# Seven products in every block pair, alternating groups, and derived factors made ahead into DRAM, in a split-weight decoder trunk

## The chip, the cores and the metric

The kernel runs on one core of a Trainium2 chip. The metric is the device time of one execution in microseconds; the time given is the median of several runs.

## The reference

Two decoder layers over 256 tokens of width 2048, all in float32:

```python
for layer in range(2):
    mix = short_conv_mixer(h, ...)        # layer 0: gated convolution of width 3, w_in 2048x6144, w_out 2048x2048
    # layer 1: latent attention, 16 heads, with low-rank projections, rotary part and output projection w_o
    h = layer_norm(ALPHA * h + mix, ...)
    f = jnp.square(jax.nn.relu(h @ w1[layer])) @ w2[layer]     # w1 2048x8192, w2 8192x2048
    h = layer_norm(ALPHA * h + f, ...)
```

The two MLPs hold most of the work: each multiplies by 2048x8192 and by 8192x2048.

## The kernel before, in words

**Weights in two parts.** To keep float32 accuracy, each weight is used as the sum of a high and a low part. SP loads it in tiles of 128x1024 (512 KB) into a ring of five (`RAW`), ScalarE copies it into the high part (L127), VectorE subtracts that from the weight and gets the low part (L128). High and low parts live in two rings of eight (`WA`). A product (`dot`, L300 to L303) is then three matmuls: high by high, low by high, high by low.

All weights form one list, `stream`, in the order in which they are used. `take` hands out the next of it and runs the preparation (`prepare`, a generator of one step for a plain tile and three for a unit of a seven-product pair) a few steps ahead (`LOOK` = 5). The instructions are written in this way and then put in order for each engine by a scheduler; each engine works through its own queue in order.

**The MLP.** The 8192 hidden columns are worked in eight groups q. In each q, `products` computes eight blocks of 128 hidden columns for all 256 tokens (L215, L219), their squares follow, and the second half of q, "down", multiplies them by the q's 1024 rows of w2. In the first and the last q, this is plain. In the six between (`FAST`), hidden blocks are taken in pairs and token halves too, which gives products of 2x2 blocks, and such a product is done in seven multiplications instead of eight (a form of Strassen and Winograd, `fast_products`). The left factors S1 to S4 are made from the hidden blocks (L707 to L710). The right factors T1 to T4 are made from the weights: a unit is two raw tiles, holding blocks 11 and 22, 21 and 12. VectorE derives T1 and T3 together into a third tile (L162, 128x1024), then T2 (L166) and T4 (L169, both 128x512), and all of them are split as above.

The 2048 output columns of w2 form two groups of two column blocks. In group 0 all four pairs of a q are seven-product pairs; in group 1, worked first, the pairs are `MIXED = "sssp"`: three seven-product pairs and a plain one of eight products.

**The sums.** Each group has its sums of products, kept in SBUF between the q's and in eight PSUM banks while they are worked: ScalarE copies a sum into its bank before the products (`resumed`, L612) and back afterwards (`put_back`, L616); some are added into SBUF by VectorE (`keep`, L624) instead. `fold` puts the parts together at the end.

**Around the MLPs.** Ahead of the first stand the opening (first tiles of x and of w_in, loaded as `lead` and `first`, split a piece at a time), the rest of w_in with the convolution (`cbuf`, whose edges GpSimd clears, L557), and w_out; between the MLPs, the latent projections, attention and w_o. GpSimd does hardly anything else.

Of the kernel before, what the change touches and what calls it, by code (L numbers as in the profile page):

```python
# [10 lines left out]
F32 = mybir.dt.float32  # L11
F32R = mybir.dt.float32r
AF = mybir.ActivationFunctionType
ALU = mybir.AluOpType
# [22 lines left out]
FAST = range(1, NQ - 1)  # L37
MIXED = "sssp"
EVEN = (QC - 1, "22")
FIRST = (0, 1, 2, 3, 4, 6, 8, 12, 16)  # L40
# [5 lines left out]
LAG = 8  # L46
WO_G = 3
BEHIND = (2, 2, 2, 3, 2, 2, 3)

# [4 lines left out]
def trunk(ctx: ExitStack, tc: tile.TileContext, xT, vecs, lead, w_first, w_in, w_out, w_kv, w_q, w_uk, w_uv,  # L54
# [18 lines left out]
    def halves(w):  # L73

        lead = len(w.shape) - 2
        return [(w,)] if lead == 0 else [h for i in range(w.shape[0]) for h in halves(w[i])]

    stream = []
    for m in range(NC):
# [19 lines left out]
    stream += halves(w_o) + mlp_stream(1)  # L99

    class Banks:
# [39 lines left out]
    def prepare(i):  # L141

        if len(stream[i]) == 1:
# [4 lines left out]
            return  # L148
        r1, r2 = (load_raw(f"{i}_{j}", src) for j, src in enumerate(stream[i]))
        out = []  # L150

        def finished(r, name):
            hi, lo = parts(name)
            split(hi, lo, tiled(r))
            out.append((hi, lo))

        b22, (b21, b12) = r1[:, BW:], (r2[:, :BW], r2[:, BW:])
        finished(r1, f"{i}_1")
# [10 lines left out]
        nc.vector.tensor_tensor(t4, b21, b12, ALU.subtract)  # L169
        f = state["fast"].tile([P, 2, BW], F32R, tag="t4", name=f"t4_{i}", bufs=2)  # L170
        split(f[:, 0, :], f[:, 1, :], t4)
        b1, t13, b2 = ([[v.rearrange("p b c -> p (b c)")[:, o:o + BW] for v in w] for o in (0, BW)] for w in out)
        ready[i] = {"11": b1[0], "22": b1[1], "21": b2[0], "T2": b2[1], "T1": t13[0], "T3": t13[1],
                    "T4": [f[:, 0, :], f[:, 1, :]]}
        yield
# [7 lines left out]
    def take(halves=2, look=LOOK):  # L183

        i = state["next"]
        state["next"] += halves
        ahead = -sum(size(j) for j in range(i, i + halves))
        for j in range(i, len(stream)):
            for step in range(size(j)):
                ahead += 1  # L190
                if ahead > look:
                    return [ready.pop(i + k) for k in range(halves)]
# [6 lines left out]
        return [ready.pop(i + k) for k in range(halves)]  # L199

# [87 lines left out]
    def products(n, x, turned=None, banks=(None,)):  # L288

        for i in range(n):  # L290
            w = take()
            ps = psum("ps_u", banks[i % len(banks)])
            mm_run([(w, ps)], x, 0, NC, NC, turned=None if i else turned)
            yield ps
# [47 lines left out]

    def fast_products(ps, x, forms, j, fresh, ready, onto=()):

# [157 lines left out]

    def summed(ln, pss, add, m0=0):

        for m, ps in enumerate(pss, m0):
            add(ps, m)
            ln.count(m)
            ln.wide(m)
# [37 lines left out]
    pss = chain(opening(xhl), lagged(3 * NC - HEAD, xhl))  # L546
    ln = Norm(0, ALPHA)
    for m in range(NC):
        part = []
# [18 lines left out]
        if m >= NC // 2:  # L568
            for k in range(2 * m - NC, 2 * m - NC + 2):
                ln.prepare(k)  # L570
    nc.sync.dma_start(id_t, ident)
    ln.widen("a1", "a2")
    summed(ln, chain(products(1, z), lagged(NC - 1, z)), residual)

    def mlp(idx, ln, blocks, fast, begin=None, extra=None, last=False):
# [39 lines left out]
        def put_back(p, g, ps):  # L615
            nc.scalar.copy(place(p, g), ps)  # L616
# [9 lines left out]
        def resume(busy, free, ps, m):  # L626

            b2, b3, b4, b6 = free
            b1, b5, b7, b22 = busy
            for p, bank in {3: (("3", b3),), 4: (("2", b2),), 5: (("4", b4), ("1", b1)), 6: (("6", b6), ("5", b5)),  # L630
                            7: (("7", b7), ("22", b22))}.get(m, ()):
                ps[p] = resumed(p, 1, f"ps_r{p}", bank)

        def down_pairs(h, forms, busy, free, ps):

            b2, b3, b4, b6 = free
            b1, b5, b7, b22 = busy
            new = set(OWN) if q == FAST[0] else set()
            onto = set(ps) - new
            for j, kind in enumerate(MIXED):  # L640
                if kind == "s":
                    last = j == MIXED.rindex("s")
                    fast_products(ps, h, forms, j, new if j == 0 else (), OWN if last else (), onto)
                    if last:
                        for p in OWN:
                            put_back(p, 1, ps[p])
                        then = {p: resumed(p, 0, f"ps_f{p}", bank) for p, bank in (("3", b1), ("1", b5))}
                    continue
                for two in (((0, "2"), (1, "4")), ((1, "22"), (0, "3"))):
                    w, = take(1, LOOK + 1)  # L650
                    for t, p in two:
                        for kk in range(2):
                            k = 2 * j + kk
                            dot(ps[p], wide_rows(w, kk), held(h[k], t), False, k == QC - 1, (k, p) == EVEN, True)
                    if j == len(MIXED) - 1:
                        if "5" not in then:
                            then.update({p: resumed(p, 0, f"ps_f{p}", bank) for p, bank in (("5", b7), ("7", b6))})
                        for _, p in two:
                            put_back(p, 1, ps[p])
            n = QC // 2  # L660
            onto = set(then) - new
            then.update({p: psum(f"ps_f{p}", bank) for p, bank in (("2", b2), ("6", b4), ("4", b22))})
            for j in range(n):
                fast_products(then, h, forms, j, set(then) - onto if j == 0 else (), then if j == n - 1 else (), onto)
            for p, _, _ in FACTORS:
                (put_back if p in onto or p in new else keep)(p, 0, then[p])
            return (b3, b1, b5, b7), (b6, b2, b4, b22)

# [16 lines left out]

        busy, free = (0, 1, 2, 3), (4, 5, 6, 7)
        for q in range(NQ):
# [54 lines left out]
            else:  # L742
                folds = fold()
                begun = {}
                for m, ps in enumerate(products(QC, xhl, TURNED, busy)):
                    hidden(m, ps, whole)
                    if extra and m == 0 and q <= NB:
                        for t in range(2):
                            extra(block, q - 1, t, busy[2 + t])
                    if q in FAST:  # L750
                        resume(busy, free, begun, m)
                    if q == NQ - 1:
                        next(folds, None)
                        if last and m >= QC - 2:
                            for t in range(2):
                                last_sum(m - QC + 2, t, free[2 * (m - QC + 2) + t])
                        if begin:
# [15 lines left out]
            else:  # L773
                busy, free = down_pairs(h, forms, busy, free, begun)

# [28 lines left out]


    with tc.tile_pool(name="att", bufs=1) as ap:
        lat = act.tile([P, 2 * NK, 2 * T], F32R, tag="c", name="lat")
# [92 lines left out]
        with tc.tile_pool(name="att2", bufs=2) as a2, \  # L900
# [107 lines left out]
            for s, n in enumerate(BEHIND, H - 4):  # L1008
                together(s)
                for _ in range(n):  # L1010
                    next(outs)
# [8 lines left out]
    after.widen("a1", "a2")  # L1020
    summed(after, out_chunks(), residual)

# [165 lines left out]
```

## Time and profile before

| | |
|---|---|
| median of 3 runs | 2000.02 us (1996.99 to 2000.58) |
| profiled execution, span | 1994.9 us |
| matmuls (records) | 11110, busy 1987.7 us |
| VectorE busy | 1709.4 us, 86% |
| ScalarE busy | 1354.9 us, 68% |
| moved by DMA | 385.85 MB, mean 193 GB/s |

The profile gives the span of the execution that it recorded; what lies around it is not given, and the median of the timed runs is 5.1 us above it. The stages, in microseconds of that execution: opening from 5, rest of w_in and convolution from 28, w_out from 273, first MLP from 362 (its six `FAST` q's from 453, 83 each), latent projections and attention from 1044, w_o from 1205, second MLP from 1304 (its `FAST` q's from 1395, 84 each) to the end. A line of the timeline reads: start, duration, engine, line of the code, operation, output and input tiles, shape; in brackets how long the engine was idle before and what ended that.

### The profile page before, as it was taken

Reading aid. Unit: us, or ns where it says so; the run is one execution under the profiler, and the core shown is the slowest. Engines: PE = TensorE matmul, PEld = TensorE weight load, DVE = VectorE, ACT = ScalarE, POOL = GpSimd, SP = SyncE. Lnnn points to the kernel's source line nnn. Section 1 sums busy time; section 2 is a strip of 40 time slices with the busy share of each in tenths; the row PEclk is TensorE's granted clock in tenths of the full one; section 3 lists DMA queues with packets and bytes.
Section 4 is the critical chain, followed back from the end, with each engine's and each line's share of the span. In section 5 each row is a group of like instructions: output and inputs, shape, how many; then the busy total and the mean of one; then the engine's idle time right before and its main releaser. Section 6 shows DMA issues by size and latency. Waiting matters only on the chain.

```text
span 1994.9 us, 30180 instructions
## 1 busy us (share of the span) xinstructions
PE 1987.7 (100%) x11110; PEld 1737.2 (87%) x11110; DVE 1709.4 (86%) x2555; ACT 1354.9 (68%) x2154; POOL 2.3 (0%) x21
## 2 busy tenths in 40 slices
PE   9999999999999999999999999999999999999998
PEld 8888888988888888888889998898888888888886
DVE  8667667797999989989978988777899999999985
ACT  6444445586778778777756755558677787887772
POOL 0000000000000000000000000000000000000000
PEclk9999999999999999999999999999999999999999
DMA  8666666565657466574855543656464656656483
GB/s 318 205 191 187 190 190 190 179 193 157 212 170 251 148 216 221 177 243 147 281 171 159 170 140 123 201 180 195 146 233 155 232 161 220 222 178 233 150 269 130
DMA packets 106853, 385.85 MB, mean 193 GB/s; under 512 B 11857, under 2 KB 12625, under 8 KB 106449
## 3 DMA queue, kind: packets, MB, share of 16 engines
q1 hardware_dynamic: 106560, 383.79, 59.5%
q8 instruction: 87, 1.43, 0.3%
q14 instruction: 62, 0.50, 0.1%
q10 hardware_dynamic: 144, 0.13, 0.0%
HBM read 381.78 MB, written 2.10 MB: 192 GB/s over the span
## 4 chain that ended last, share of the span: by engine, by line
PE 98%; DVE 1%; ACT 1%; issue 0%; DVEq 0%; ACTq 0%
PE ps_u L215 20%; PE ps_l L215 13%; PE ps_u L219 10%; PE ps_l L219 7%; PE ps_f L300 4%; PE ps_f L303 4%; PE ps_f L302 4%; PE ps_r L303 4%; PE ps_r L302 4%; PE ps_r L300 4%; PE ps_d L300 2%; PE ps_d L302 2%; PE ps_d L303 2%; PE ps_w L249 2%; PE ps_w L248 2%; PE ps_w L247 2%
## 5 line engine op out<-in xcount | busy, mean ns | idle before, releaser
L128 DVE TENSOR_TENSOR lo<-raw,hi 128x1024 fp32r<-128x1024 f32 x710 | 861.8, 1220 | 190.6 <-ACT hi L127 119.9
L127 ACT CAST hi<-raw 128x1024 fp32r<-128x1024 f32 x710 | 741.8, 1051 | 247.4 <-PE ps_l L215 98.1
L215 PE MATMUL ps_u<-xhl,hi 128*128 128x512 f32 x1792 | 621.7, 392 | 0.0
L219 PE MATMUL ps_u<-xhl,lo 128*128 128x256 f32 x1792 | 498.2, 279 | 0.0
L215 PEld LDWEIGHTS ps_u<-xhl,hi 128*128 128x128 f32 x1792 | 334.5, 187 | 73.6 <-ACT acc L595 0.2
L219 PEld LDWEIGHTS ps_u<-xhl,lo 128*128 128x128 f32 x1792 | 338.1, 189 | 1.8
L215 PE MATMUL ps_l<-xhl_a,hi 128*128 128x512 f32 x704 | 244.1, 393 | 0.0
L219 PE MATMUL ps_l<-xhl_a,lo 128*128 128x256 f32 x704 | 195.4, 279 | 0.0
L215 PEld LDWEIGHTS ps_l<-xhl_a,hi 128*128 128x128 f32 x704 | 132.1, 188 | 29.9
L219 PEld LDWEIGHTS ps_l<-xhl_a,lo 128*128 128x128 f32 x704 | 131.9, 188 | 0.2
L127 ACT CAST hi_t<-raw_t 128x1024 fp32r<-128x1024 f32 x84 | 88.5, 1054 | 45.8 <-DVE raw_t L162 41.4
L162 DVE TENSOR_TENSOR raw_t<-raw,raw 128x1024 f32<-128x1024 f32 x84 | 102.3, 1218 | 1.8 <-DMA raw<-in_w2f_dram 1.5
L128 DVE TENSOR_TENSOR lo_t<-raw_t,hi_t 128x1024 fp32r<-128x1024 f32 x84 | 102.4, 1219 | 0.2
L718 ACT ACTIVATE fp<-fp 128x256 f32<-128x256 f32 x96 | 40.0, 416 | 63.2 <-DVE fp L356 62.6
L215 PE MATMUL ps_l<-z,hi 128*128 128x512 f32 x240 | 82.4, 391 | 0.0
L300 PE MATMUL ps_d<-hi,h 128*128 128x512 f32 x192 | 75.0, 391 | 0.0
L302 PE MATMUL ps_d<-lo,h 128*128 128x512 f32 x192 | 75.0, 390 | 0.0
L303 PE MATMUL ps_d<-hi,h 128*128 128x512 f32 x192 | 74.8, 389 | 0.0
L249 PE MATMUL ps_w<-xd,hi 128*128 128x258 f32 x256 | 72.7, 284 | 0.0
L248 PE MATMUL ps_w<-xd,lo 128*128 128x258 f32 x256 | 72.3, 282 | 0.0
L247 PE MATMUL ps_w<-xd,hi 128*128 128x258 f32 x256 | 72.3, 282 | 0.0
L215 PE MATMUL ps_l<-oT,hi 128*128 128x512 f32 x208 | 71.3, 391 | 0.0
(296 smaller groups left out, 3963.7 us busy)
## 6 DMA issues: line engine op xcount, KB each, us to landing
raw<-in_w_dram SPq DMA_DIRECT2D x344, 512.0 KB, 4.5
raw<-in_w2f_dram SPq DMA_DIRECT2D x168, 512.0 KB, 3.9
raw<-in_w_in_dram SPq DMA_DIRECT2D x88, 512.0 KB, 4.2
raw<-in_w_out_dram SPq DMA_DIRECT2D x32, 512.0 KB, 3.7
raw<-in_w_o_dram SPq DMA_DIRECT2D x32, 512.0 KB, 4.2
raw<-in_w_kv_dram SPq DMA_DIRECT2D x10, 512.0 KB, 3.7
raw<-in_w_q_dram SPq DMA_DIRECT2D x8, 512.0 KB, 4.0
raw<-in_w_uk_dram SPq DMA_DIRECT2D x8, 512.0 KB, 3.9
```

What stands on the lines that cost most here:

```text
L127: nc.scalar.copy(hi, src)
L128: nc.vector.tensor_tensor(lo, src, hi.bitcast(F32), ALU.subtract)
L162: nc.vector.tensor_tensor(t.rearrange(two, a=2), b12.unsqueeze(1).to_broadcast([P, 2, BW]), r1.rearrange(two, a=2), ALU.subtract)
L215: nc.tensor.matmul(ps, w[blk // 8][0][:, blk % 8, :], x, start=first, stop=False)
L219: nc.tensor.matmul(ps[:, :T], w[blk // 8][1][:, blk % 8, :], x[:, :T], start=False, stop=last)
L247: nc.tensor.matmul(ps[:, :W], hi, x[k][:, :W], start=k == 0, stop=False)
L248: nc.tensor.matmul(ps[:, :W], lo, x[k][:, :W], start=False, stop=False)
L249: nc.tensor.matmul(ps[:, :W], hi, x[k][:, W:], start=False, stop=k == NC - 1)
L300: nc.tensor.matmul(ps, x[0], w[0], start=first, stop=False, skip_group_check=onto)
L302: nc.tensor.matmul(ps[:, at], x[0], w[1][:, at], start=False, stop=False, skip_group_check=onto)
L303: nc.tensor.matmul(ps, x[1], w[0], start=False, stop=last, skip_group_check=onto)
L718: nc.scalar.activation(f, f, AF.Relu)
```

## The change

All four pairs of group 1 become seven-product pairs too, so that each of the twelve `FAST` q's has eight of them. The group worked first alternates from q to q (`groups`); the first four sums of the group worked second stay in their PSUM banks into the next q. Sums 3 and 1 (`FRESH`) start anew in PSUM and are added to the sums in SBUF by VectorE; the others are copied in and out by ScalarE. `keep` now follows each product as it ends.

```diff
-MIXED = "sssp"
-EVEN = (QC - 1, "22")
+EARLY = {0: ((1, 0), (1, 2)), 1: ((1, 1),)}
+FRESH = ("3","1")
...
+MAKE_FROM = 6
...
-            for j, kind in enumerate(MIXED):
-                out += [(w2f[l, q, 1, j, 0], w2f[l, q, 1, j, 1])] if kind == "s" else \
-                    halves(w2[l, q, 2, j]) + halves(w2[l, q, 3, j])
-            out += [(w2f[l, q, 0, j, 0], w2f[l, q, 0, j, 1]) for j in range(QC // 2)]
+            for i, g in enumerate(groups(q)):
+                for j in range(QC // 2):
+                    out.append((w2f[l, q, g, j, 0], w2f[l, q, g, j, 1]) + made.get((l, q, i, j), ()))
```

For the units that `EARLY` names (two in each q of the first MLP, one in each of the second; 18 in all) the derived factors are made ahead by `making`: GpSimd loads both raw tiles, VectorE derives T1/T3, T2 and T4, GpSimd stores them in DRAM. `making(0)` is advanced during the convolution (from its step 6) and w_out, `making(1)` during attention and w_o.

```diff
+    def making(l, pool):
...
+            for r, src in zip((r1, r2), w2f[l, q, groups(q)[i], j]):
+                nc.gpsimd.dma_start(r, src)
+            yield
...
+            nc.vector.tensor_tensor(t.rearrange(two, a=2), b12.unsqueeze(1).to_broadcast([P, 2, BW]),
+                                    r1.rearrange(two, a=2), ALU.subtract)
+            nc.vector.tensor_tensor(r1[:, :BW], b22, t[:, :BW], ALU.subtract)
+            nc.vector.tensor_tensor(r1[:, BW:], b21, r1[:, :BW], ALU.subtract)
+            nc.gpsimd.dma_start(to13, t)
+            nc.gpsimd.dma_start(to24, r1)
```

When its turn comes, such a unit loads four tiles (one of them half as wide) on SP and is only split:

```diff
+        if len(stream[i]) == 4:
+            r1, t13 = load_raw(f"{i}_0", stream[i][0]), load_raw(f"{i}_1", stream[i][2])
+            finished(r1, f"{i}_1")
+            yield
+            t24 = load_raw(f"{i}_2", stream[i][3])
+            b21 = raws.tile([P, 1024], F32, tag="raw", name=f"raw{i}_3")[:, :BW]
+            nc.sync.dma_start(b21, stream[i][1][:, :BW])
+            finished(t13, f"{i}_t")
+            yield
+            finished(t24, f"{i}_2")
+            ready[i] = {**named((("11", "22"), ("T1", "T3"), ("T2", "T4"))), "21": fourth(b21)}
```

The preparation is now also advanced in the middle of a unit, by one or two steps (`spent`), in `products` after half of a block and in `fast_products` after products 1 and 7:

```diff
         for p, l, r in FACTORS:
             dot(ps[p], b[r], a[l], p in fresh, p in ready, onto=p in onto)
+            if p in "17":
+                spent("17".index(p) + 1)
+            if then:
+                then(p)
```

In `down_pairs` the sums follow the new order of groups:

```diff
-        def resumed(p, g, name, bank):
+        def begun_sum(p, g, name, bank):
             ps = psum(name, bank)
-            if q != FAST[0] or p not in OWN:
+            if not new_sum(p):
                 nc.scalar.copy(ps, place(p, g))
             return ps
-        def keep(p, g, ps):
+        def keep(p, g, ps, since):
             at = place(p, g)
-            if q == FAST[0] and p in OWN:
+            if p not in FRESH or (since == FAST[0] and p in OWN):
                 nc.scalar.copy(at, ps)
             else:
                 nc.vector.tensor_tensor(at, at, ps, ALU.add)
...
+            for j in range(n):
+                if j == n - 1:
+                    begin_next(order[0], spare)
+                fast_products(ps, h, forms, j, new - held_on if j == 0 else (), ps if j == n - 1 else (),
+                              set(ps) - (new - held_on), turn if j == n - 1 else None)
             for j in range(n):
-                fast_products(then, h, forms, j, set(then) - onto if j == 0 else (), then if j == n - 1 else (), onto)
...
+                fast_products(after, h, forms, j, new if j == 0 else (), after if j == n - 1 else (),
+                              set(order) - new, end if j == n - 1 else None)
```

More of the change, by code (lines that the diff above doesn't have):

```diff
@@ L155, in finished, with fourth, named @@
             out.append((hi, lo))
+        def fourth(src):
+            f = state["fast"].tile([P, 2, BW], F32R, tag="t4", name=f"t4_{i}", bufs=2)
+            split(f[:, 0, :], f[:, 1, :], src)
+            return [f[:, 0, :], f[:, 1, :]]
+        def named(names):
+            return {n: [v.rearrange("p b c -> p (b c)")[:, o:o + BW] for v in w]
+                    for w, pair in zip(out, names) for n, o in zip(pair, (0, BW))}
+        if len(stream[i]) == 4:
[9 more added lines that the diff above has]
+            ready[i] = {**named((("11", "22"), ("T1", "T3"), ("T2", "T4"))), "21": fourth(b21)}
+            yield
+            return
+        r1, r2 = (load_raw(f"{i}_{j}", src) for j, src in enumerate(stream[i]))
         b22, (b21, b12) = r1[:, BW:], (r2[:, :BW], r2[:, BW:])
@@ L169, in prepare @@
         nc.vector.tensor_tensor(t4, b21, b12, ALU.subtract)
[L170 to L174, printed above, removed]
+        ready[i] = {**named((("11", "22"), ("T1", "T3"), ("21", "T2"))), "T4": fourth(t4)}
         yield
@@ L186, in take, with spent @@
         state["next"] += halves
-        ahead = -sum(size(j) for j in range(i, i + halves))
+        state["taken"] = i, sum(size(j) for j in range(i, i + halves))
+        spent(0, look)
+        return [ready.pop(i + k) for k in range(halves)]
+    def spent(n, look=LOOK):
+        i, total = state["taken"]
+        ahead = -total
         for j in range(i, len(stream)):
@@ L190, in take @@
                 ahead += 1
-                if ahead > look:
-                    return [ready.pop(i + k) for k in range(halves)]
+                if ahead > look + n:
+                    return
                 if j < 2 * HEAD:
@@ L684, in last_sum @@
             nc.scalar.copy(finals[n, t], block(n, t))
-        busy, free = (0, 1, 2, 3), (4, 5, 6, 7)
+        busy, sums_in, places = (0, 1, 2, 3), {}, {"3": 4, "1": 5, "5": 6, "7": 7}
         for q in range(NQ):
@@ L773, in mlp @@
             else:
-                busy, free = down_pairs(h, forms, busy, free, begun)
+                busy, sums_in, places = down_pairs(h, forms, sums_in, places, busy[3])
     def to_wide(block, put, h):
```

114 lines of the change are left out of this document (65 added, 49 removed).

## The prediction

> **What bounds the kernel now.** I read the page's engine totals and its chain first, then the windows by stage, then single instructions on the timeline.
>
> ```profile
> span 1994.9 us, 30180 instructions
> PE 1987.7 (100%) x11110; PEld 1737.2 (87%) x11110; DVE 1709.4 (86%) x2555; ACT 1354.9 (68%) x2154; POOL 2.3 (0%) x21
> PE 98%; DVE 1%; ACT 1%; issue 0%; DVEq 0%; ACTq 0%
> ```
>
> PE is busy throughout and carries 98% of the chain. VectorE is next, at 86%; since that is an average over stages, I read it by stage. The rows below hold, as us and (x instructions), PE, PEld, DVE, ACT and POOL, then the granted clock, the share of the DMA engines and GB/s: one whole group q of the first MLP, its second half (the down products), one whole q of the second MLP, a stretch inside the first, the opening, and the convolution stage.
>
> ```profile
> 536.00:619.20 83.20, 83.20 (x429) 71.28 (x428) 78.09 (x101) 66.44 (x104) 0.00 (x0) 1.00 0.60 199
> 580.40:619.20 38.80, 38.80 (x174) 32.15 (x173) 38.63 (x46) 31.30 (x46) 0.00 (x0) 1.00 0.58 184
> 1562.70:1646.80 84.10, 84.10 (x437) 71.87 (x437) 79.72 (x104) 66.50 (x103) 0.00 (x0) 1.00 0.60 198
> 564.70:615.10 50.40, 50.40 (x246) 42.61 (x245) 50.13 (x69) 39.84 (x63) 0.00 (x0) 1.00 0.47 147
> 4.00:24.00 20.00, 20.00 (x116) 17.64 (x116) 16.66 (x41) 15.85 (x42) 0.00 (x0) 1.00 1.00 388
> 16.00:18.00 2.00, 2.00 (x12) 1.62 (x12) 1.38 (x3) 2.00 (x4) 0.00 (x0) 1.00 1.03 434
> 27.90:273.10 245.20, 245.20 (x1413) 215.10 (x1412) 167.99 (x248) 115.32 (x155) 1.39 (x14) 1.00 0.66 202
> ```
>
> Three things follow. PE never waits in a q. VectorE is full in the down half (38.63 of 38.80) and over the longer stretch (50.13 of 50.40): there the margin is not VectorE's average but how far ahead of PE it has split the weights. And from 4 to 24 us the DMA engines are full (share 1.00); the most that any window here moved is 434 GB/s.
>
> The margin itself is read on the timeline: when VectorE ends a low part, and when PE first uses it.
>
> ```profile
> 563.48 1.23 DVE L128 TENSOR_TENSOR lo<-raw,hi 128x1024 fp32r<-128x1024 f32 x1 [0.83 <-ACT hi L127]
> 580.40 0.39 PE L300 MATMUL ps_r<-hi,forms 128*128 128x512 f32 x1
> 580.63 0.40 PE L302 MATMUL ps_r<-lo,forms 128*128 128x512 f32 x1
> 611.32 1.22 DVE L162 TENSOR_TENSOR raw_t<-raw,raw 128x1024 f32<-128x1024 f32 x1
> 612.57 0.69 DVE L166 TENSOR_TENSOR raw<-raw,raw_t 128x512 f32<-128x512 f32 x1
> 613.30 0.69 DVE L169 TENSOR_TENSOR raw<-raw 128x512 f32<-128x512 f32 x1
> 613.91 1.22 DVE L128 TENSOR_TENSOR lo_t<-raw_t,hi_t 128x1024 fp32r<-128x1024 f32 x1
> 615.04 1.22 DVE L128 TENSOR_TENSOR lo<-raw,hi 128x1024 fp32r<-128x1024 f32 x1
> 616.18 0.68 DVE L128 TENSOR_TENSOR t<-raw,t 128x512 fp32r<-128x512 f32 x1
> 616.78 2.35 DVE L128 TENSOR_TENSOR lo<-raw,hi 128x1024 fp32r<-128x1024 f32 x2
> 616.06 0.39 PE L302 MATMUL ps_f<-lo_t,forms 128*128 128x512 f32 x1
> 1641.22 1.22 DVE L128 TENSOR_TENSOR lo_t<-raw_t,hi_t 128x1024 fp32r<-128x1024 f32 x1
> 1643.66 0.39 PE L302 MATMUL ps_f<-lo_t,forms 128*128 128x512 f32 x1
> ```
>
> The first low part of this q's down products ends at 563.48 + 1.23 = 564.71 and is used at 580.63: 15.92 us ahead, which the ring of eight split tiles allows. The factor T1/T3 of the last pair ends at 613.91 + 1.22 = 615.13 and is used at 616.06: 0.93 us ahead. In the second MLP's q it is 1643.66 − 1642.44 = 1.22 us. So each q eats its whole lead and ends about a microsecond short of stalling.
>
> **The change, part by part.**
>
> *Products.* The one plain pair of the twelve FAST q's (six in each MLP) becomes a seven-product pair: eight dots become seven, each of three matmuls. Two matmuls start 580.63 − 580.40 = 0.23 us apart. So 12 × 3 × 0.23 = **−8.3 us**, all on PE's path.
>
> *VectorE in the down stretch.* From starts above, a 1024 split takes 615.04 − 613.91 = 1.13 us and a 512 one 616.78 − 616.18 = 0.60. A seven-product pair costs VectorE four of the first kind and three of the second, 6.3 us; the plain pair cost two splits, 2.26. The exchange adds 4.1 us of VectorE work inside the stretch from the first low part to the last T1/T3. A unit whose factors were made ahead lacks one 1024 and two 512 operations: −2.3. There are two such units in a q of the first MLP, one in a q of the second. Two VectorE additions to sums kept in SBUF, which ended a q before, now fall inside the stretch: +1.2. That makes +4.1 − 4.6 + 1.2 = +0.7 us in the first MLP and +3.0 in the second, while PE's part of the stretch gets 0.7 shorter. VectorE has 0.27 us idle over this stretch (50.40 − 50.13), so nothing absorbs it. The leads become 0.93 − 0.7 − 0.7 = −0.5 and 1.22 − 3.0 − 0.7 = −2.5.
>
> *The made units' loads.* Such a unit loads three 512 KB tiles and a part of one instead of two, through the same ring of five.
>
> ```profile
> raw<-in_w2f_dram SPq DMA_DIRECT2D x168, 512.0 KB, 3.9
> L127 ACT CAST hi<-raw 128x1024 fp32r<-128x1024 f32 x710 | 741.8, 1051 | 247.4 <-PE ps_l L215 98.1
> ```
>
> The third load is issued only when the unit before has given up a buffer; with 3.9 us to land and 1.05 for ScalarE's high part it needs 5.0 us, against four VectorE splits (4 × 1.13 = 4.5) until VectorE wants it: about 0.5 us idle a unit, 1.0 a q in the first MLP and 0.5 in the second. Bounds: 0 if the ring runs a step further ahead, 3.9 if the load starts when it is wanted.
>
> Together PE waits 0.5 + 1.0 = 1.5 us a q in the first MLP and 2.5 + 0.5 = 3.0 in the second. The next products stage (580.4 − 536.0 = 44.4 us of PE against 78.09 − 38.63 = 39.5 of VectorE) refills the lead, so this recurs but does not pile up: 6 × 1.5 + 6 × 3.0 = **+27**; of this I take **+24**, since the refills in mid-pair that the change adds let some splits start earlier. Bounds: 0 to 6 × (1.5 + 3.0) + 12 = 39, with another microsecond in each q. ScalarE hides the copies that go away (66.44 of 83.20 us busy): no gain.
>
> *Making in the opening.* The code asks for the derived factors from the seventh step of the convolution on. But in the order of the built program GpSimd's first four loads of 512 KB stand right behind its first two memsets and wait for nothing, and VectorE's first derivation stands eighth on its engine, ahead of the second opening split; what is queued behind that wait is the opening's splits, and PE waits for those.
>
> ```profile
> 0.73 0.14 POOL L557 MEMSET cbuf<- 128x2 f32 x2 [0.29 <-POOLq L1175]
> 15.96 2.18 ACT L127 CAST hi<-first 128x512 fp32r<-128x512 f32 x4 [1.45 <-DMA first<-in_w_first_dram]
> 16.64 3.93 PE L215 MATMUL ps_g<-xhl_a,hi 128*128 128x512 f32 x16
> 19.81 2.18 ACT L127 CAST hi<-first 128x512 fp32r<-128x512 f32 x4 [0.71 <-DMA first<-in_w_first_dram]
> ```
>
> GpSimd is free at 0.87 us, and the opening's own tiles come just in time: ScalarE waits 1.45 and 0.71 us for them, and PE uses one 0.68 us after its split begins. So every byte more delays PE: 2.1 MB at 388 to 434 GB/s is 4.8 to 5.4 us. The next two units add up to 2.1 MB of stores and loads. I take **+7**; bounds 0 (GpSimd's packets yield) and 11. The Trainium skill ("DMA: Bandwidth & Descriptors", section "Issuing engines are not separate DMA queues") says that DMAs of sync, scalar and gpsimd run on the same 16 engines and interleave, so another issuing engine saves only issue time. By that rule the full 2.1 MB lie on PE's path and the lower bound of 0 falls away; a path of its own for GpSimd would give 2023.7 − 7 = 2016.7 us. No run so far shows two queues loaded at once.
>
> *Making later.* The other eleven units of the first layer stand on VectorE, in the new order, between the instructions of these two rows of before.
>
> ```profile
> 23.75 3.78 DVE L128 TENSOR_TENSOR lo<-raw,hi 128x1024 fp32r<-128x1024 f32 x3 [0.78 <-ACT hi L127]
> 106.11 0.48 DVE L563 SCALAR_TENSOR_TENSOR cbuf<-cbuf,vec 128x256 f32<-128x256 f32 x1
> ```
>
> They move 2.1 MB each (two loads, two stores), 23 MB in 82 us: 280 GB/s on top of the stage's own 202, above the 434. With the 232 GB/s that are free they take 100 us, 18 late. VectorE's work there is no limit: 245 − 168 = 77 us idle in the stage against 12 × 2.3 = 28. A late unit holds up the splits queued behind it, and PE once the splits made ahead are used; those reached 15.92 us ahead in the q above, nearly the 18, so I take **+1**, bounds 0 and 18. The second layer's six units fall into the last q and attention, 14 us of VectorE in all: +0, at most 4.
>
> Sum on the profiled execution: 1994.9 − 8.3 + 24 + 7 + 1 = 2018.6. The median of the runs, 2000.02, stands 5.1 above that span, so I forecast **2023.7 us**, +1.2%.
>
> **The rivals.**
>
> *Everything is hidden (faster).* GpSimd's packets yield in the opening, or PE makes up for it, and splits run ahead far enough through the mid-pair refills that no lead falls under zero. Then only the products change: 2000.0 − 8.3 = **1991.7 us**. For it: the first MLP's lead is short by only 0.5, and a q's VectorE total still lies below PE's. Against: the second MLP's deficit is 2.5 us with VectorE at 50.13 of 50.40. The time is below before's as long as stalls and opening together cost less than 8.3.
>
> *Only the opening costs.* −8.3 + 7 + 1: **1999.7 us**, no change. For it: the same small deficits. Against: as above.
>
> *The convolution stage becomes DMA-bound.* The 18 us come on PE in full, because the opening's delay leaves no splits ahead: 17 more than in the sum, **2041 us**. For it: 280 + 202 is over 434. Against: a late unit lets SP's loads run alone meanwhile, and the ring fills.
>
> *The change does not relieve VectorE*, because the third load of made units comes late each time (the 3.9 us bound): 18 × 3.4 = 61 more, partly instead of deficits: **2075**. That it does not save the dots is excluded: the order of the built program has them gone.
>
> **How the numbers follow.** A measurement of this kernel can tell about 0.2% (4 us) from no change: 1996 to 2004. My forecast has 0.58, with its own range 2012 to 2042 (stalls from the second MLP's deficit alone, 6 × 2.5 = 15, to 39; opening 4.8 to 11). Everything hidden: 0.17. Only the opening: 0.10, of which 0.02 falls below 1996. Convolution stage: 0.11. Loads late: 0.04. So faster 0.19, same 0.08, slower 0.73. The range 1996 to 2043 leaves out the hidden case below, and the late loads above.
>
> **What would show it.** In the profile after: PE's matmuls down by 36 in the down products; idle of PE at lo_t or hi_t of the last pairs, about twice as long in the second MLP as in the first, VectorE full before it. The stage starts: the convolution starting near 35 instead of 27.9 us, with a DMA share of 1 and GpSimd's queue in it. I am wrong if the opening starts its second stage on time, or if each q of the second MLP takes 83.4 us or less, or if the convolution stage is much longer than 245 us.

## The result, and the profile after

The changed kernel takes **2068.46 us** (median of 4 runs, 2064.66 to 2069.73) against 1999.59 for the kernel before: a ratio of 1.0342, 95% interval 1.0327 to 1.0356. The forecast was 2023.7, range 1996 to 2043: the direction was right, the size was three times too small and the range missed. The profiled execution of the changed kernel spans 2065.7 us, 70.8 more than before's.

From the page of the changed kernel: the span, the engines' busy time, the engines' shares of the chain, and GpSimd's DMAs with their median time to landing.

```profile
span 2065.7 us, 30280 instructions
PE 2011.7 (97%) x11062; PEld 1735.1 (84%) x11062; DVE 1746.3 (85%) x2605; ACT 1335.6 (65%) x2094; POOL 41.1 (2%) x93
PE 49%; DVE 25%; DMA 12%; issue 8%; ACT 5%; POOL 1%; SPq 0%; DVEq 0%; ACTq 0%; POOLq 0%
m<-in_w2f_dram POOLq DMA_DIRECT2D x36, 512.0 KB, 7.2
made<-m POOLq DMA_DIRECT2D x36, 512.0 KB, 6.0
```

PE still shows as 97% busy, but it carries only 49% of the chain, where it carried 98%; VectorE has 25% and DMA 12%. When a busy share looks unchanged, the chain shows what changed. The windows that answer to those of before: the opening, the convolution, one whole q of the first MLP, its down half, and one whole q of the second MLP.

```profile
4.00:30.80 26.80, 21.45 (x116) 18.81 (x116) 20.40 (x46) 16.05 (x42) 2.69 (x5) 0.94 1.02 401
34.69:302.00 267.31, 253.41 (x1412) 220.20 (x1411) 190.00 (x280) 114.39 (x156) 21.82 (x52) 0.97 0.81 266
568.82:654.32 85.50, 83.65 (x425) 70.35 (x424) 77.64 (x100) 65.51 (x98) 0.00 (x0) 1.00 0.66 216
613.21:654.32 41.11, 39.26 (x170) 31.23 (x169) 37.24 (x44) 30.82 (x43) 0.00 (x0) 1.00 0.59 193
1535.00:1623.00 88.00, 85.66 (x434) 72.27 (x434) 81.31 (x105) 64.68 (x98) 0.00 (x0) 0.98 0.62 202
```

PE's busy time is now below the window's length in every one of them. The stage lengths (us), from the first matmul of each stage, are of the one profiled execution of each kernel; the runs of one kernel lie up to 11 us apart, and `gated` was profiled in its fastest run, `seven_old_sums` in its slowest, so the medians are given with both; an MLP counts from its first FAST q to its end. The stages not listed (w_out, the q's ahead of the FAST ones) differ by 0.2 at most unless a section says so:

| kernel | opening | convolution | 1st MLP | latent, attention | w_o | 2nd MLP | span |
|---|---|---|---|---|---|---|---|
| before | 22.7 | 245.2 | 591.0 | 161.2 | 99.3 | 600.3 | 1994.9 |
| changed | 29.5 | 267.3 | 612.2 | 165.0 | 99.3 | 617.1 | 2065.7 |
| no_making | 22.9 | 245.2 | 613.0 | 161.2 | 99.3 | 622.2 | 2039.1 |
| gated | 23.2 | 245.5 | 610.0 | 161.9 | 99.2 | 617.1 | 2053.6 |
| loads_early | 28.0 | 245.2 | 613.0 | 161.2 | 99.3 | 617.1 | 2039.2 |
| no_spent | 30.6 | 265.3 | 613.9 | 163.3 | 99.3 | 629.0 | 2076.8 |
| no_t4 | 22.9 | 245.2 | 589.3 | 161.2 | 99.3 | 601.0 | 1994.2 |
| pool_t4 | 23.3 | 245.2 | 637.9 | 161.2 | 99.3 | 648.0 | 2090.2 |
| fresh_none_nomake | 23.3 | 245.2 | 608.7 | 161.2 | 99.3 | 616.1 | 2028.8 |
| seven_old_sums | 23.0 | 245.2 | 617.4 | 161.3 | 99.3 | 626.2 | 2047.7 |
| placed | 23.0 | 245.2 | 603.8 | 161.2 | 103.6 | 615.4 | 2027.5 |
| placed_three | 22.7 | 245.2 | 597.9 | 161.2 | 102.9 | 614.1 | 2019.4 |
| placed_three_fresh | 23.2 | 245.2 | 601.3 | 161.2 | 105.0 | 613.4 | 2024.5 |
| more | 22.8 | 245.2 | 597.0 | 187.9 | 118.5 | 609.9 | 2056.3 |

So the 70.8 us are: opening 6.8, convolution 22.1, first MLP 21.2 (16.0 in its FAST q's and 5.2 in its last q), attention 3.8, second MLP 16.8. The stages in which factors are made cost 38 us, the FAST q's 33.

### The profile page after: what moved, and what is told of

It is laid out like the page before. It is cut to its first block, busy times and chain, and to the rows that moved or that the text cites. A ratio compares the mean times of both kernels' runs of the same rounds, so it can differ in the third digit from the quotient of the medians.

```text
span 2065.7 us, 30280 instructions
## 1 busy us (share of the span) xinstructions
PE 2011.7 (97%) x11062; PEld 1735.1 (84%) x11062; DVE 1746.3 (85%) x2605; ACT 1335.6 (65%) x2094; POOL 41.1 (2%) x93
## 4 chain that ended last, share of the span: by engine, by line
PE 49%; DVE 25%; DMA 12%; issue 8%; ACT 5%; POOL 1%; SPq 0%; DVEq 0%; ACTq 0%; POOLq 0%
PE ps_l L268 10%; PE ps_u L268 8%; DVE lo L157 7%; DMA raw<-in_w2f_dram 5%; PE ps_l L272 5%; PE ps_u L272 4%; DVE lo_t L157 4%; DVE raw_t L213 4%; DMA m<-in_w2f_dram 3%; DMA raw<-in_w_dram 2%; ACT hi L156 2%; DVE raw L217 2%; DVE raw L220 2%; DVE t L157 1%; PE ps_w L302 1%
## 5 line engine op out<-in xcount | busy, mean ns | idle before, releaser
L157 DVE TENSOR_TENSOR lo<-raw,hi 128x1024 fp32r<-128x1024 f32 x710 | 859.0, 1219 | 158.9 <-ACT hi L156 123.7
L268 PE MATMUL ps_l<-xhl_a,hi 128*128 128x512 f32 x704 | 250.5, 400 | 0.0
L272 PE MATMUL ps_l<-xhl_a,lo 128*128 128x256 f32 x704 | 199.1, 285 | 13.9 <-DVE lo L157 13.9
L156 ACT CAST hi_t<-raw_t 128x1024 fp32r<-128x1024 f32 x78 | 82.1, 1052 | 105.4 <-DVE raw_t L213 89.3
L272 PEld LDWEIGHTS ps_l<-xhl_a,lo 128*128 128x128 f32 x704 | 135.0, 192 | 16.3 <-DVE lo L157 16.1
L213 DVE TENSOR_TENSOR raw_t<-raw,raw 128x1024 f32<-128x1024 f32 x78 | 95.0, 1217 | 5.5 <-DMA raw<-in_w2f_dram 5.4
L157 DVE TENSOR_TENSOR lo_t<-raw_t,hi_t 128x1024 fp32r<-128x1024 f32 x78 | 95.0, 1218 | 2.5 <-ACT hi_t L156 2.2
L156 ACT CAST t<-raw 128x512 fp32r<-128x512 f32 x96 | 59.3, 618 | 30.2 <-DMA raw<-in_w2f_dram 19.1
L355 PE MATMUL ps_f<-hi_t,forms 128*128 128x512 f32 x176 | 69.6, 404 | 8.6 <-ACT ps_f L689 5.3
L157 DVE TENSOR_TENSOR t<-raw,t 128x512 fp32r<-128x512 f32 x96 | 65.8, 685 | 11.0 <-ACT t L156 11.0
L302 PE MATMUL ps_w<-xd,hi 128*128 128x258 f32 x256 | 73.1, 286 | 0.0
L301 PE MATMUL ps_w<-xd,lo 128*128 128x258 f32 x256 | 72.9, 285 | 0.0
```

Source lines behind the costliest of these rows:

```text
L156: nc.scalar.copy(hi, src)
L157: nc.vector.tensor_tensor(lo, src, hi.bitcast(F32), ALU.subtract)
L213: nc.vector.tensor_tensor(t.rearrange(two, a=2), b12.unsqueeze(1).to_broadcast([P, 2, BW]), r1.rearrange(two, a=2), ALU.subtract)
L268: nc.tensor.matmul(ps, w[blk // 8][0][:, blk % 8, :], x, start=first, stop=False)
L272: nc.tensor.matmul(ps[:, :T], w[blk // 8][1][:, blk % 8, :], x[:, :T], start=False, stop=last)
L301: nc.tensor.matmul(ps[:, :W], lo, x[k][:, :W], start=False, stop=False)
```

## The experiments

Two theories. **Split lead**: in the q's VectorE has more work than the lead of split weights covers (the prediction's arithmetic), and making costs what its bytes cost. **In-order waits**: loads that land late hold up what is queued behind them on VectorE or ScalarE. Both turn out to hold in part: the first in the q's of the kernels without made units, the second where factors are made and where made units are loaded. The L numbers are lines of each run's own kernel; a row of waits ends in the total us, how many there were, and the longest.

**No making** (`no_making`).

```diff
-EARLY = {0: ((1, 0), (1, 2)), 1: ((1, 1),)}
+EARLY = {}
```

> No factor is made ahead (the list of early units is empty); the seven-product pairs, the alternating groups and the refills in mid-unit stay. Both theories: the opening ends near 28 us again, the convolution stage takes 245 us again, the last q of the first MLP and attention lose 9 us, in all 38 us less than the changed kernel's 2065.7. They differ in the FAST q's. Split lead (the prediction's arithmetic): VectorE has 4.6 us (first MLP) and 2.3 us (second) more in each down stretch, so PE's stalls grow from about 3.4 us a q to 5 or more, together 20 us or more: span about 2040. Late loads in order: the stalls came from the made units' own loads, on which ScalarE waits with the copies of sums behind it; with them gone the stalls fall under 1.5 us a q, and the span is about 2000.

Measured: 2041.16 us, ratio 1.0210 (1.0195 to 1.0225), span 2039.1. Making's stages recover as both expected; the FAST q's get longer (the second MLP by 5.1 us; the first by 0.8 although its last q gets back 5), and the span is the 2040 of the split lead, not the 2000 of late loads. In its q from 540.39 (second row: the down half) VectorE is busy 41.47 of 41.75 us, and over the first MLP PE waits for high parts, hi_t (which follows VectorE's raw_t) before all.

```profile
540.39:626.41 86.02, 84.65 (x426) 69.86 (x425) 81.96 (x106) 65.20 (x98) 0.00 (x0) 1.00 0.59 196
584.66:626.41 41.75, 40.38 (x172) 30.81 (x170) 41.47 (x50) 30.19 (x43) 0.00 (x0) 1.00 0.45 149
PE ps_f L355 <- ACT hi_t L156: 4.9, 6, 1.0
PE ps_f L355 <- ACT hi L156: 3.3, 11, 0.5
```

**Making tied to its places, loads and derivations** (`gated`): two small operations before each pair of loads make the loads wait for the convolution's newest output.

```diff
+            if "gate" in state:
+                for r in (r1, r2):
+                    nc.vector.tensor_tensor(r[:, :T], state["gate"], state["gate"], ALU.mult)
             for r, src in zip((r1, r2), w2f[l, q, groups(q)[i], j]):
                 nc.gpsimd.dma_start(r, src)
...
+                state["gate"] = xres[:, m, :]
...
+            state["gate"] = y
```

> The first layer's making waits for the place that the code asks for: two small VectorE operations (128x256) that read the convolution's newest output stand before each unit's two loads, so the first unit loads in step 6 of the convolution and the others follow one a step. The amount moved is the same. If the bytes themselves are the cost (DMA engines full), the convolution stage still loses most of its 22 us; if the cost is VectorE standing in order behind loads that have not landed, a derivation now stands behind several splits, and both the opening (29.5 to 22.7 us) and the convolution (267 to about 246) recover: span about 2037. The FAST q's should not change.

Measured: 2063.55 us, ratio 1.0315 (1.0293 to 1.0337), span 2053.6 in the fastest of its runs (2055.37 to 2066.0), not the 2037 expected. Opening and convolution recover, but w_out, which follows, grows from 88.9 to 110.2 us. The derivation still comes too soon after its load: VectorE waits over 5 us in each step (first row, from the timeline). The lead of the splits hides that until PE needs the last output of the convolution (second row, from the waits between 262 and 300 us).

```profile
267.71 1.23 DVE L126 TENSOR_TENSOR m<-m,m 128x1024 f32<-128x1024 f32 x1 [5.55 <-DMA m<-in_w2f_dram]
PE ps_u L271 <- DVE z L423: 16.8, 1, 16.8
```

**Early loads, late derivations** (`loads_early`).

```diff
+            if "gate" in state:
+                nc.vector.tensor_tensor(t[:, :T], state["gate"], state["gate"], ALU.mult)
             nc.vector.tensor_tensor(t.rearrange(two, a=2), b12.unsqueeze(1).to_broadcast([P, 2, BW]),
                                     r1.rearrange(two, a=2), ALU.subtract)
...
```

The gate is set as in `gated`; the loads are left free to go early, as far as there are buffers.

> GpSimd's first four loads (2.1 MB) stay where they are, at the start of the opening, but VectorE's derivations wait for the convolution's step 7 and later (a 128x256 operation on the target tile that reads the convolution's newest output). If the opening's 6.8 us were the 2.1 MB sharing the DMA engines (the prediction's price), the opening still takes 28 us or more instead of 22.7. If they were VectorE waiting for those loads ahead of the opening's splits, it takes 23 to 24. Convolution as in the gated kernel, about 246; span about 2037 or 2043.

Measured: 2040.34 us, ratio 1.0203 (1.0186 to 1.0220), span 2039.2. Its opening and convolution, then a derivation from its timeline:

```profile
4.00:29.30 25.30, 21.57 (x115) 18.61 (x115) 17.46 (x41) 16.74 (x42) 0.54 (x1) 1.00 1.01 397
33.34:278.51 245.17, 245.17 (x1412) 215.05 (x1411) 188.40 (x280) 115.23 (x155) 18.66 (x46) 1.00 0.79 266
149.26 1.22 DVE L125 TENSOR_TENSOR m<-m,m 128x1024 f32<-128x1024 f32 x1
```

This separates the two costs. In the opening VectorE waits for no made load any more, and the opening still takes 28.0: 5.3 of the 6.8 us are the 2.1 MB that share full DMA engines (share 1.01). In the convolution the same mean of 266 GB/s as in the changed kernel cost PE nothing, 245.17 of 245.17 us busy: there it was the place of the derivations. Their place also sets when most loads run, since a load waits for a buffer that a derivation frees; what that means is taken up again below.

**No refills in mid-unit** (`no_spent`).

```diff
-            if p in "17":
-                spent("17".index(p) + 1)
```

(and `spent(1)` in `products`)

> The changed kernel without the refills in mid-unit: the preparation is advanced only at each take, as before the change. The prediction gave these refills 3 us of gain in all (27 to 24). Split lead: stalls of the FAST q's grow by up to 0.5 us each, 6 in all, span 2066 to 2072. If the refills do harm, because they put more split work ahead of the copies of sums in ScalarE's order, the span falls by a few us, 2058 to 2066.

Measured: 2078.5 us, ratio 1.0403 (1.0386 to 1.0421), span 2076.8. The refills are worth 11 us, nearly all of it in the second MLP (617.1 to 629.0; the first 612.2 to 613.9).

**T4 not derived** (`no_t4`) and **derived by GpSimd** (`pool_t4`), both without making.

```diff
-        nc.vector.tensor_tensor(t4, b21, b12, ALU.subtract)
+        t4 = b22                                                # no_t4
+        nc.gpsimd.tensor_tensor(t4, b21, b12, ALU.subtract)     # pool_t4
```

> Base: the kernel without making (span 2039.1). The subtraction that derives T4 (VectorE, 128x512, 0.60 us, eight a q) is left out; block 22 is split in T4's place, so all other instructions stay. VectorE has 4.8 us less in each FAST q. If VectorE's amount of work in the down products is what PE waits for, the 52 us of stalls above 1994.9 - 8.2 = 1986.7 nearly vanish (12 x 4.8 = 58): span 1987 to 1995. If it is the chain raw_t, hi_t, lo_t that goes back and forth between VectorE and ScalarE, its latency stays and the span stays over 2030.

Measured: 1997.27 us, ratio 0.9986 (0.9976 to 0.9996), span 1994.2, with T4's derivation left out. 4.8 us less VectorE work in a q takes 45 us off the span of 2039.1 (24 in the first MLP, 21 in the second), so in the kernel without made units VectorE's amount of work is what PE waits for. The same q as above, whole and down half, with PE busy throughout and VectorE no longer full:

```profile
536.49:619.35 82.86, 82.86 (x426) 70.54 (x425) 76.86 (x98) 65.26 (x97) 0.00 (x0) 1.00 0.62 200
580.88:619.35 38.47, 38.47 (x171) 31.36 (x170) 36.69 (x43) 30.42 (x42) 0.00 (x0) 1.00 0.53 164
```

> Base: the kernel without making (span 2039.1). The same subtraction is done by GpSimd, which is idle there, instead of VectorE; nothing is left out. Work bound: VectorE is relieved as in the kernel without T4, and if GpSimd takes under 2 us for it the span comes near 1990, faster than before. If GpSimd's operation slows VectorE's (shared access) or takes 3 us or more, the split of T4 is late and holds up both ScalarE and VectorE in order: 2020 to 2060.

Measured: 2089.38 us, ratio 1.0451 (1.0435 to 1.0468). GpSimd takes 1.56 us for the operation, and some of VectorE's operations get slower beside it. From the groups of this kernel, then two of the same groups in the changed one; after the count stand the busy us, the mean ns of one, and the idle us before them:

```profile
L220 POOL TENSOR_TENSOR raw<-raw 128x512 f32<-128x512 f32 x96 | 149.6, 1558 | 1561.4 <-DVE lo L157 745.8 <-DMA raw<-in_w2f_dram 348.0 <-DVE raw L217 217.1
L157 DVE TENSOR_TENSOR lo_t<-raw_t,hi_t 128x1024 fp32r<-128x1024 f32 x96 | 147.4, 1536 | 18.9 <-ACT hi_t L156 18.9
L776 DVE TENSOR_TENSOR sf<-sf,fp 128x128 f32<-128x128 f32 x48 | 34.5, 719 | 0.8
```

```profile
L157 DVE TENSOR_TENSOR lo_t<-raw_t,hi_t 128x1024 fp32r<-128x1024 f32 x78 | 95.0, 1218 | 2.5 <-ACT hi_t L156 2.2
L776 DVE TENSOR_TENSOR sf<-sf,fp 128x128 f32<-128x128 f32 x48 | 13.7, 285 | 0.4
```

The split of T1/T3, which comes right after, goes from 1218 to 1536 ns, and one of the S operations from 285 to 719 (`no_making`, this kernel's base, has 1219 and 285). The operation taken off VectorE was 66 us there (96 of 687 ns); the two groups above add 51 (30 and 21), and the plain splits, 1256 ns in place of 1219, another 26. The relief is more than eaten up; what else goes into the 48 us over `no_making` was not separated. The Trainium skill ("SBUF — State Buffer", section "SBUF: two separate sides") says that a VectorE operation with two SBUF inputs and a GpSimd operation that reads SBUF lock each other out for the whole instruction; the longer rows agree.

**All sums copied, none added** (`fresh_none_nomake`, without making): `FRESH = ()`.

> Base: the kernel without making (span 2039.1). No sum starts anew and is added by VectorE; all are copied in and out by ScalarE. VectorE has two 128x512 additions (1.2 us) less in a FAST q, ScalarE two copies in (1.2 us) more. Work of VectorE as the bound: 12 x 1.2 = 14 us less, 2025. ScalarE's copies at the change of groups as the bound: they get later, 2040 to 2055.

Measured: 2030.92 us, ratio 1.0161 (1.0146 to 1.0176), span 2028.8. 10.3 us less than without it, of 14 expected: VectorE's work again.

**The pair alone** (`seven_old_sums`): the kernel before with only its plain pair replaced, and the sums' banks fitted to that.

```diff
-MIXED = "sssp"
+MIXED = "ssss"
...
+            for j in range(n):
...
+                fast_products(ps, h, forms, j, new if j == 0 else (), order if j == n - 1 else (), onto)
+            for p, nxt, bank in zip(order, order[1:] + [None], (b3, b1, b5, b7, b2, b6, None)):
+                put_back(p, 1, ps[p])
...
```

> The kernel before with nothing but its plain pair replaced by a seven-product pair: no alternating groups, no refills in mid-unit, no making; all seven sums of the first group are copied in and out by ScalarE as before. Split lead, by the prediction's arithmetic: VectorE +4.1 us in the down stretch against a lead of 0.9 to 1.2, PE 0.7 shorter: about 3.7 us of stall a q, 44 in all, less 8.2: 1994.9 + 36 = 2031. If the pair itself is harmless and the new arrangement of the sums is what costs: 1987 to 1995.

Measured: 2046.1 us, ratio 1.0225 (1.0203 to 1.0247), span 2047.7 in the slowest of its runs (2040.14 to 2049.47). The pair alone costs 47 us by the medians (1999.05 before), 53 in the profiled execution; 36 were expected. So the pair is what costs, and the new arrangement of sums and the refills together give back about 5 by the medians (`no_making` is 42 above before), 8.6 by the spans.

**Repairs**: `placed` ties the first two units' loads and every derivation to their places; `placed_three` stores T1/T3 and 21/T2, so that a made unit loads three tiles; `placed_three_fresh` adds `FRESH = ()`; `more` adds to that 30 made units in place of 18.

```diff
+                if l == 0 and q == FAST[0]:                                                    # placed
+                    nc.vector.tensor_tensor(r[:, :T], state["gate"], state["gate"], ALU.mult)
...
+            nc.vector.tensor_tensor(t[:, :T], state["gate"], state["gate"], ALU.mult)
...
-            nc.gpsimd.dma_start(to24, r1)                                                      # placed_three
+            nc.gpsimd.dma_start(to24, r2)
...
-            b21 = raws.tile([P, 1024], F32, tag="raw", name=f"raw{i}_3")[:, :BW]
-            nc.sync.dma_start(b21, stream[i][1][:, :BW])
...
+            t4 = r1[:, :BW]
+            nc.vector.tensor_tensor(t4, t24[:, :BW], t24[:, BW:], ALU.subtract)
...
+EARLY = {0: ((0, 3), (1, 0), (1, 2)), 1: ((1, 0), (1, 2))}                                     # more
...
+MAKE_FROM = 1
...
```

> The changed kernel with making tied to its places: 128x256 VectorE operations that read the newest convolution output stand before the first two units' loads and before every derivation, so that the loads start after the opening and land well before VectorE comes to the derivation; in the second layer the derivations are tied to attention. In order waits of VectorE as the cost of making: opening 29.5 to 23, convolution 267.3 to 245.2, last q of the first MLP and attention 9 less, span 2065.7 - 6.6 - 22.1 - 9 = 2028. The FAST q's stay at 516 and 520 us. If a part of these costs were the bytes, it stays: the convolution at 250 or more.

Measured: 2033.03 us, ratio 1.0168 (1.0153 to 1.0183), span 2027.5. Opening, convolution, last q and attention are back at before's, for 4.3 us in w_o. The convolution moves 275 GB/s, against 266 in the changed kernel, and PE does not wait:

```profile
28.39:273.56 245.17, 245.17 (x1413) 215.07 (x1411) 189.46 (x284) 114.85 (x155) 20.72 (x50) 1.00 0.82 275
```

> The same, but a made unit stores T1/T3 and the pair 21/T2, so that it loads three full tiles instead of three and a half (four buffers of the ring of five), and VectorE derives T4 from 21 and T2 (one 128x512 operation, 0.6 us more than before for each such unit: 1.2 a q in the first MLP, 0.6 in the second). If the fourth buffer and its late load eat the relief of the made units, the q's get shorter by 1 us or more each in spite of it: span about 2010 to 2018. If VectorE's amount alone counts, they get longer by up to 1.2 and 0.6: span about 2033 to 2038.

Measured: 2021.65 us, ratio 1.0116 (1.0099 to 1.0133), span 2019.4 (2010 to 2018, or 2033 to 2038, were expected). The first MLP gets 5.8 us shorter although VectorE does 1.2 us more in each q: there the fourth tile ate the relief, by its late landing or by its buffer. The second gets 1.3 shorter in spite of 0.6 more in each q, where 1 us a q was expected.

> The kernel with three loads, and no sum is added by VectorE (all copied by ScalarE). Without making this gave 10.3 us. Work of VectorE as the bound: about 10 us less than the kernel with three loads. If ScalarE's order is what PE waits for once made units are there, no gain or a loss of up to 10.

Measured: 2025.14 us, ratio 1.0129 (1.0113 to 1.0146), span 2024.5: no gain, against the work-bound expectation. The first MLP loses 3.3 us, w_o 2.1, and the second MLP gains 0.6 with some 7 us less VectorE work (two additions of 0.60 a q): once made units are there, VectorE's amount alone does not set the time.

> The same again with 30 made units instead of 18: three in each q of the first MLP, two in each of the second; making starts at step 1 of the convolution and runs through attention. Each unit saves VectorE 1.7 us of its q, one more unit in every q. Work bound: the stalls fall by up to 12 x 1.7 = 20 us against the kernel before it, span near 1995 to 2000, if the second layer's making costs attention nothing; it may cost 10, as VectorE waits there in order.

Measured: 2055.82 us, ratio 1.0285 (1.0269 to 1.0300), span 2056.3, where 1995 to 2000 was expected. The MLPs fall by 8 us in all and not 20; making in attention and w_o costs 27 and 13 us over the kernel without the added units. No version tried, with the whole computation, is faster than the kernel before.

## Why the prediction was wrong

In the terms of the prediction's sum, the 70.8 us are −8.3 (products) + 41 (stalls in the q's) + 7 (opening) + 22 (convolution) + 9 (second layer's making); the forecast had −8.3 + 24 + 7 + 1 + 0. The convolution is the step that failed most; the stalls and the second layer follow.

**Products, −8.3: right as arithmetic, never seen.** The records of matmuls fall by 48, four a q where the forecast counted three, since one product of the plain pair was done in four matmuls (`two`, L301 of before). Even where VectorE is relieved by 4.8 us (`no_t4`), the q above is 82.86 against 83.20 us, and the two MLPs together are 1.0 us shorter than before's, of 8.3: small waits remain.

**VectorE in the down stretch: right for units that are not made.** Its arithmetic gave spans of about 2040 for `no_making` and 2031 for `seven_old_sums`; measured were 2039.1 and 2047.7, and taking VectorE's work away takes the stalls away. In the changed kernel it does not hold. VectorE is not full there (37.24 of 41.11 us in the down half above, where before had 38.63 of 38.80), and the two MLPs stall alike (20 and 21 us, as worked out next), where the forecast had the second twice as long.

**Made units' loads: under-sized, and by another way.** The FAST q's grew by 32.8 with 8.3 us saved: stalls of 41 us, where the prediction had 24 (8 in the first MLP, 16 in the second; measured 20 and 21). The prediction let VectorE wait for the third load, 0.5 us a unit. In the trace ScalarE waits, and for the fourth, which also needs a buffer of the ring of five. In the second MLP PE waits almost only for copies of sums on ScalarE (from the waits between 1420 and 1960 us):

```profile
PE ps_f L355 <- ACT ps_f L689: 9.6, 7, 2.2
```

Three rows of the changed kernel, from ScalarE's and PE's timeline:

```profile
1517.93 0.62 ACT L156 CAST t<-raw 128x512 fp32r<-128x512 f32 x1 [1.49 <-DMA raw<-in_w2f_dram]
1518.46 0.58 ACT L689 COPY ps_f<-acc 128x512 f32<-128x512 f32 x1
1519.09 0.50 PE L355 MATMUL ps_f<-hi,h 128*128 128x512 f32 x1 [1.23 <-ACT ps_f L689]
```

The split of block 21 waits 1.49 us for its load, the copy of a sum into its bank stands behind it, and PE waits 1.23 us for that copy. "ScalarE hides the copies" looked at a busy share of 66 of 83 us; a copy behind a late load is on the path at any share. `placed_three`, without that load, confirms it for the first MLP (5.8 us). In the second it brought 1.3, and less VectorE work on top of that 0.6 (`placed_three_fresh`), so what sets the rest of the 21 us there stays open.

**Refills, 3 us: they are worth 11**, nearly all in the second MLP.

**Opening, +7: right**, 6.8. The bytes cost 5.3 (`loads_early`) where the estimate was 4.8 to 5.4. The rule of the Trainium skill ("DMA: Bandwidth & Descriptors", section "Issuing engines are not separate DMA queues") that was set beside it agrees: GpSimd's loads did not yield. The rest is the in-order wait that the prediction named: VectorE's first derivation waits for its load, and PE for the split behind it.

```profile
10.52 1.22 DVE L123 TENSOR_TENSOR m<-m,m 128x1024 f32<-128x1024 f32 x1 [4.61 <-DMA m<-in_w2f_dram]
12.22 1.19 PE L268 MATMUL ps_g<-xhl_a,hi 128*128 128x512 f32 x2 [5.35 <-DVE xhl_a L598]
```

**Convolution, +1: the step that failed**, by 21 us, above its own upper bound of 18; a convolution much longer than 245 us was one of its signs of being wrong. The sum compared bytes with what the DMA engines have free, got 18 us of lateness, and let a lead of 15.92 us, read in a q of the MLP, take it up. But the bytes alone do not make PE wait. While the first layer's factors are made, `placed` (second row) moves them at nearly the same rate as the changed kernel (first row), with DMA engines as full, and PE is busy throughout:

```profile
34.69:158.00 123.31, 109.41 (x584) 93.84 (x583) 84.19 (x121) 44.35 (x61) 20.81 (x44) 0.95 0.93 326
146.00:273.50 127.50, 127.50 (x737) 111.96 (x736) 106.25 (x162) 57.42 (x78) 18.14 (x39) 1.00 0.91 321
```

What differs is when VectorE comes to a derivation. In the changed kernel that is before its loads have landed, and they are late by a chain of latencies: GpSimd's next load waits for the store that frees one of two buffers, 6.0 us to land, then 7.2 for the load, and VectorE stands in order before it. Why these take longer than SP's loads (4.3 to 4.9 us) was not tried. From the waits between 34.69 and 302 us:

```profile
DVE m L123 <- DMA m<-in_w2f_dram: 27.0, 6, 7.0
POOL m L119 <- DMA made<-m: 25.5, 8, 7.1
PEld ps_l L272 <- DVE lo L157: 16.1, 7, 4.7
PE ps_l L272 <- DVE lo L157: 13.9, 6, 4.4
```

So VectorE was held up for at least 27.0 us where the sum had 18, and the splits made ahead took up about half of it. PE's waits of 13.9 us (16.1 with its weight loads) became 22.1, mostly because the clock falls after the four longer ones, at some 1.6 us each. Three windows of 5 us around a wait of 3.18 us, which ends at 110.19:

```profile
105.00:110.00 5.00, 2.01 (x12) 1.47 (x10) 2.56 (x3) 1.69 (x3) 1.07 (x2) 1.00 0.98 383
110.00:115.00 5.00, 4.82 (x19) 4.11 (x19) 4.03 (x6) 1.32 (x2) 1.36 (x3) 0.66 1.01 370
115.00:120.00 5.00, 5.00 (x30) 4.38 (x29) 2.61 (x3) 1.05 (x1) 0.24 (x1) 1.00 1.02 355
```

In the middle one the granted clock is 0.66 and PE gets through 19 matmuls where the next one has 30. The rival that gave 2041 had the right stage and, with 18 us, nearly the size; its mechanism, engines too full, does not make PE wait by itself, as `placed` shows.

**Second layer's making, +0, at most 4: 9.0.** The forecast priced VectorE's work there (14 us, hidden) and not its waits. Three of the six units fall into the last q of the first MLP, where VectorE waits for their loads and PE for 3.5 us at once; tied to attention they cost 4.3, in w_o (`placed`). Why w_o pays was not tried.

## What to carry to other kernels

An operation that waits for a load is priced by what is queued behind it on its in-order engine, and by the latency chain that lets the load start, not by bytes or busy shares alone: bytes moved at the same rate cost 22 us or nothing, depending on where the consumer stood. Before work is moved off a saturated engine "for later", see where the scheduler puts it and tie both the load and its consumer to their places. A saving on the bounding engine is worth nothing when the next engine has less than that to spare over the stretch in which its lead is used up.

## What the runs showed that was not expected

In the changed kernel each of the eight waits of PE of 2.0 us and more after the first 8 us (2.00, 2.09, 2.24, 3.18, 3.37, 3.49, 4.43 and 5.35 us) goes with a stretch of 3.4 us, from near its end on, in which the granted clock is 0.50: matmuls of 512 columns start 0.43 us apart instead of 0.23, so that such a wait costs some 1.6 us on top. After waits of 1.6 us and less, in the same kernel, it stays at 1.00. The wait of 2.00 us ends at 143.53, one of 1.56 us at 1952.12:

```profile
144.98:148.40 3.42, 3.42 (x12) 2.86 (x12) 2.25 (x4) 0.00 (x0) 0.47 (x2) 0.50 0.90 281
1952.00:1957.00 5.00, 4.88 (x21) 3.75 (x22) 4.27 (x6) 5.00 (x10) 0.00 (x0) 1.00 0.71 243
```

The Trainium skill ("TensorE: Matmul & The Clock Gate", Part 1) has a free-running window of about 3.4 us, and half the clock after at least one idle window. Half rate and the 3.4 us agree with it; the waits of 2.00 to 2.24 us, shorter than such a window, were enough here, and the measurement decides.
